# Issuing the transposes of an older attention block ahead of the new block's logits

## The chip, the cores and the metric

The kernel runs on one core of one Trainium2 chip. The metric is device microseconds (us) of one execution. Names of engines: PE is the matrix engine (PEld its weight loads), DVE the vector engine, ACT the scalar engine, POOL the GpSimd engine, SP the engine that issues most DMAs.

## The reference

Two layers of a streaming encoder over 2048 tokens of width 1024. Layer 0 is a pooling mixer; one key/value projection follows it; layer 1 is attention with 16 heads of width 64. The change lies in the attention, which is not a softmax but "stick-breaking": a logit gives the chance to stop at a key, and the weight of a key is that chance times the product of (1 - chance) over all later keys.

```python
def stick_breaking_attention(q, k, v):
    # A[t,s] = beta[t,s] * prod_{s<j<t} (1 - beta[t,j]), beta = sigmoid(q.k / sqrt(d))
    ...
        log_keep = jnp.where(mask, jax.nn.log_sigmoid(-logits), 0.0)
        later = lax.cumsum(log_keep, axis=log_keep.ndim - 1, reverse=True) - log_keep
        log_a = jax.nn.log_sigmoid(logits) + later
        a = jnp.where(mask, jnp.exp(log_a), 0.0)
        outs.append(jnp.einsum('bhts,bhsd->bhtd', a.astype(v.dtype), v[:, :, :L]))
```

After it come the gate `o * silu(z)`, the output projection, and a gated embedding add.

## The kernel before

**Two stages.** The first stage (all dense layers up to q, k and v, and the copies of the later weights to DRAM in split form) ends at about 1410 us of the span; the change does not touch it. The second stage is the attention with the dense work that is left.

**Attention blocks.** The sequence is cut into four chunks of 512 tokens. The list `slots` runs over query chunks c from 3 down to 0, over 16 heads, and over key chunks from c down to 0. A slot is a 512x512 block of one head: 64 slots for c=3, 48 for c=2, 32 for c=1 and 16 for c=0. The slot with equal query and key chunk is called diagonal; there only the causal part is worked on. A slot has four steps, one for each 128 query rows, so there are 640 steps, counted by n from 0.

**What a step issues.** The loop at L809 to L842 issues four things for a step n:

- `front` (L591), the logits of step n: two matmuls (L598, L599) into a `psl` buffer, ACT's sigmoid (L602) into a `kap` buffer; in a diagonal slot POOL's causal select (L604) on it. `front` hands back `scan`: DVE's running product over the keys (L609), which writes `pp`.
- `turn` (L617), the transposes of the block that is `LAG_T` = 6 steps back: up to four transposes on PE (L623) of the `pp` tiles into a `psa` buffer, ACT's copy (L626), and DVE's subtraction (L627) that gives the rest of the split (`at`). It works on four scans of an earlier slot at a time, so its latest input is the scan three steps back.
- the filler: pieces of the dense products that are left (`piecewise`, L661: matmuls L664, L666, L668), `rate` of them per step: 3 with c=3, then 441/176, 441/112 and 441/48 for c=2, 1 and 0. Behind a finished product stand DVE, ACT and POOL instructions (L705 to L708, L729 to L732, L751 to L756).
- `gather` (L630), for the block `LAG_G` = 8 steps back: two matmuls (L635, L636) of `at` with v into `pso`; at the end of a head an ACT copy, a DVE addition, and for every second head a multiplication on POOL (L640 to L648).

**Buffers.** The product tiles lie in PSUM with two buffers for each of `psl`, `psa`, `pso` and `psd`. So the transposes of one step have to wait until the subtraction L627 of two steps earlier has read its `psa` buffer.

**Order.** Each engine works through its own queue in order. The tile framework's scheduler sets the order in each queue at build time: it starts from the order in which the code issues instructions, and lets one go ahead of another where it reckons that this one is ready sooner. What stands in the queues can be printed from the built program.

Of the kernel before, what the change touches and what calls it, by code (L numbers as in the profile page):

```python
# [29 lines left out]
def f(ap):  # L30
    return ap.bitcast(F32)
# [3 lines left out]
def trunk_kernel(ctx, tc, x, p, a_norm, a_w_in, a_w_group, a_scale, a_w_out, kv_norm, w_kv,  # L35
# [509 lines left out]
    with ExitStack() as st:  # L545
# [45 lines left out]
        def front(st, j):  # L591

            w = (j + 1) * P if st["diag"] else W5
            r0 = W5 - w
            ps = psl.tile([P, W5], F32, tag="psl", name="psl")
            qs = slice(j * P, (j + 1) * P)
            (qa, qb), kk = st["q"], st["k"]
            T.matmul(ps[:, :w], qa[:, qs], kk[:, :w], start=True, stop=False)  # L598
            T.matmul(ps[:, :w], qb[:, qs], kk[:, :w], start=False, stop=True)  # L599
            kp = kaps[kcount[0] % NK]  # L600
            kcount[0] += 1
            A.activation(out=kp[:, r0:], in_=ps[:, :w], func=AF.Sigmoid, scale=-1.0)  # L602
            if st["diag"]:
                G.affine_select(out=kp[:, W5 - P :], in_=kp[:, W5 - P :], pattern=[[-1, P]], compare_op=ALU.is_gt,  # L604
                                fill=1.0, base=0, channel_multiplier=1)

            def scan():
                pp = t2.tile([P, W5], F32, tag="pp", name="pp", bufs=12)
                V.tensor_tensor_scan(out=pp[:, r0:][:, ::-1], data0=kp[:, r0:][:, ::-1],  # L609
                                     data1=zeros.to_broadcast([P, w]),  # L610
                                     initial=1.0 if st["diag"] else st["carry"][j], op0=ALU.mult, op1=ALU.add)
                st["carry"][j] = pp[:, r0 : r0 + 1]
                st["a"].append((pp, r0))

            return scan

        def turn(st, kt):  # L617

            j0 = kt if st["diag"] else 0
            pt = psa.tile([P, W5], F32, tag="psa", name="psa")  # L620
            for j in range(j0, 4):
                pp, r0 = st["a"][j]
                T.transpose(pt[:, j * P : (j + 1) * P], pp[:, r0 + kt * P : r0 + (kt + 1) * P], ident)  # L623
            at = t2.tile([P, 2, W5], F32R, tag="at", name="at", bufs=3)
            cs = slice(j0 * P, W5)
            A.copy(out=at[:, 0, cs], in_=pt[:, cs])  # L626
            V.tensor_tensor(out=at[:, 1, cs], in0=pt[:, cs], in1=f(at[:, 0, cs]), op=ALU.subtract)  # L627
            st["at"][kt] = at

        def gather(st, kt):  # L630
            cs = slice((kt if st["diag"] else 0) * P, W5)
            if st["diag"] and kt == 0:
                st["o"].append(pso.tile([P, W5], F32, tag="pso", name="pso"))
            po, at, vv = st["o"][0], st["at"].pop(kt), st["v"]
            T.matmul(po[:, cs], vv[:, kt, :], at[:, 0, cs], start=(st["diag"] and kt == 0), stop=False)  # L635
            T.matmul(po[:, cs], vv[:, kt, :], at[:, 1, cs], start=False, stop=(st["last"] and kt == 3))  # L636
            if st["last"] and kt == 3:
                half, os, c, h2 = st["h"] % 2, st["os"], st["c"], st["h"] // 2
                mine, other = slice(half * HD, (half + 1) * HD), slice((1 - half) * HD, (2 - half) * HD)
                A.copy(out=os[mine], in_=po[other])  # L640
                V.tensor_tensor(out=os[mine], in0=po[mine], in1=os[mine], op=ALU.add)  # L641
                if half:
                    zt = t2.tile([P, W5], F32, tag="zt", name="zt", bufs=1)
                    nc.sync.dma_start(out=zt, in_=zd[c][h2])
                    for j in range(4):
                        js = slice(j * P, (j + 1) * P)
                        A.activation(out=os[:, js], in_=os[:, js], func=AF.Identity, bias=ends[c][:, h2, j : j + 1])  # L647
                    G.tensor_tensor(out=os, in0=os, in1=zt, op=ALU.mult)  # L648
                    outs[c].append(os)
# [127 lines left out]
        def beside(c):  # L777

            if c < NSUB - 1:
                yield from post(c + 1)  # L780
                return
            for cz in range(c, -1, -1):
                yield from gate_z(cz)
# [3 lines left out]
        slots = []  # L787
# [4 lines left out]
        active, filler, owed, head = {}, beside(NSUB - 1), 0.0, {}  # L792
        rate = POSTZ / 64.0
        LAG_T, LAG_G = 6, 8
# [3 lines left out]
        def begin(i):  # L798
            c, h, kc = slots[i]
            if kc == c:  # L800
                if h == 1:
                    ends[c] = load_ends(c)
                os = head["os"] if h % 2 else t2.tile([P, W5], F32, tag="os", name="os", bufs=9)
                head.clear()
                head.update(q=load_q(c, h), carry=[None] * 4, o=[], os=os)
            kk, vv = load_kv(kc, h)
            active[i] = dict(head, c=c, h=h, k=kk, v=vv, diag=kc == c, last=kc == 0, a=[], at={})

        for n in range(4 * len(slots) + LAG_G):  # L809
            i, j = divmod(n, 4)  # L810
            scan = None
            if i < len(slots):
                c, h, kc = slots[i]
                if j == 0:
                    if i == 0:
                        begin(0)
                    if i + 1 < len(slots):
                        begin(i + 1)
                scan = front(active[i], j)
            i2, j2 = divmod(n - LAG_T, 4)  # L820
            if 0 <= i2 < len(slots):
                turn(active[i2], j2)
            if scan is not None:
                scan()
            owed += rate
            while owed >= 1.0:
                next(filler, None)
                owed -= 1.0
            i3, j3 = divmod(n - LAG_G, 4)
            if 0 <= i3 < len(slots):  # L830
                gather(active[i3], j3)
                if j3 == 3:
                    st3 = active.pop(i3)
                    c3 = st3["c"]
                    if len(outs[c3]) == 8 and c3 not in done:
                        done.add(c3)
                        for _ in filler:
                            pass
                        if c3:
                            filler = beside(c3 - 1)  # L840
                            rate = POST / (64.0 * c3 - 2 * LAG_G)
                            owed = 0.0  # L842
# [31 lines left out]
```

## Time and profile before

| | before |
|---|---|
| median of 3 runs | 2869.15 us (2866.77 to 2869.49) |
| the profiled execution | 2867.54 us |
| its span | 2865.7 us |
| PE busy, share of the span | 96% |
| DVE busy | 66% (about nine tenths in the first two thirds of the attention) |
| ACT busy | 49% |
| POOL busy | 33% |
| DMA, mean | 201 GB/s |

The profile is one execution, with an instruction's start and duration on each engine. The time of a group of instructions can be added up for a stretch of the span; for a wait the profile names the instruction whose end released it. Matmuls overlap each other: the end of one is modelled, and lies after the start of the next.

### The profile page before, as it was taken

The page shows a single profiled execution, that of the slowest core. Times are in us where ns is not written, and L with a number is a line of the kernel's source. Part 1 is how long each engine was busy: PE and PEld are TensorE (multiplying, and loading weights), DVE is VectorE, ACT ScalarE, POOL GpSimd, SP SyncE. Part 2 cuts the span into 40 slices and gives each one's busy share as a digit, 9 for nine tenths or more (in the row PEclk, how much of TensorE's full clock was granted, in tenths as well). Part 3 has the DMA queues.
Part 4 walks back from the last instruction along what each step waited for, and adds up shares of the span by engine and source line. Part 5 has one row for each costly group of instructions (what it writes and reads, how often), then busy time and mean ns, then how long its engine had stood idle before and what let it go on. Part 6 is the DMA issues. An engine that isn't in the chain of part 4 may idle for free. (4 is left out here: it accounts for less than half of the span.)

```text
span 2865.7 us, 40527 instructions
## 1 busy us (share of the span) xinstructions
PE 2763.3 (96%) x13667; PEld 2273.2 (79%) x13667; DVE 1893.8 (66%) x2581; ACT 1405.6 (49%) x2765; POOL 956.2 (33%) x965
## 2 busy tenths in 40 slices
PE   8899999999999999999899999999999999999999
PEld 6688788888888888888777888787877778878877
DVE  5645535455355543555299989999999988886642
ACT  4444523355234542345255555656566655554431
POOL 3464347542474425743212121221111122213220
PEclk9999999999999999999999999999999999999999
DMA  7756696467955678446657565555555556667765
GB/s 265 257 162 216 220 305 208 143 205 250 306 160 169 223 243 287 136 153 207 212 188 229 163 216 170 159 164 177 165 161 161 163 176 193 186 188 243 251 207 158
DMA packets 335139, 576.43 MB, mean 201 GB/s; under 512 B 32782, under 2 KB 161838, under 8 KB 334932
## 3 DMA queue, kind: packets, MB, share of 16 engines
q1 hardware_dynamic: 327944, 564.34, 61.2%
q10 hardware_dynamic: 6988, 9.50, 1.1%
q8 instruction: 108, 1.77, 0.3%
q14 instruction: 99, 0.81, 0.1%
HBM read 433.16 MB, written 132.19 MB: 197 GB/s over the span
## 5 line engine op out<-in xcount | busy, mean ns | idle before, releaser
L353 PE MATMUL psd<-wpair,x 128*128 128x512 f32 x2304 | 544.8, 393 | 0.0
L602 ACT ACTIVATE kap<-psl 128x512 f32<-128x512 f32 (+3 forms) x640 | 340.3, 533 | 407.6 <-PE psl L599 398.3
L609 DVE TENSOR_TENSOR_SCAN pp<-kap,pp,zeros 128x512 f32<-128x512 f32 x384 | 512.2, 1338 | 23.3 <-ACT kap L602 21.2
L353 PEld LDWEIGHTS psd<-wpair,x 128*128 128x128 f32 x2304 | 428.8, 188 | 86.4
L623 PE MATMUL psa<-ident,pp 128*128 128x128 f32 x2176 | 348.7, 275 | 42.7 <-DVE at L627 37.9
L627 DVE TENSOR_TENSOR at<-psa,at 128x512 fp32r<-128x512 f32 (+3 forms) x640 | 373.5, 586 | 14.8 <-ACT at L626 13.8
L623 PEld LDWEIGHTS psa<-ident,pp 128*128 128x128 f32 x2176 | 263.5, 141 | 127.0 <-DVE at L627 71.2
L626 ACT CAST at<-psa 128x512 fp32r<-128x512 f32 (+3 forms) x640 | 331.3, 519 | 51.7 <-PE psa L623 48.5
L604 POOL TENSOR_SCALAR_AFFINE_SELECT kap<-kap 128x128 f32<-128x128 f32 x256 | 88.0, 345 | 633.1 <-ACT kap L602 597.9
L609 DVE TENSOR_TENSOR_SCAN pp<-kap,zeros 128x128 f32<-128x128 f32 (+3 forms) x256 | 214.2, 838 | 93.7 <-POOL kap L604 92.4
L598 PE MATMUL psl<-kk,qa 128*128 128x512 f32 (+3 forms) x640 | 235.0, 367 | 7.0 <-ACT vr L390 5.2
L635 PE MATMUL pso<-at,vv 128*128 128x512 f32 (+3 forms) x640 | 235.2, 367 | 0.8 <-ACT at L626 0.7
L599 PE MATMUL psl<-kk,qb 128*128 128x512 f32 (+3 forms) x640 | 235.1, 367 | 0.0
L636 PE MATMUL pso<-at,vv 128*128 128x512 f32 (+3 forms) x640 | 234.1, 366 | 0.0
L126 PE MATMUL psd<-xp,wpair 128*128 128x512 f32 x512 | 201.2, 393 | 4.3 <-DVE wpair L108 4.2
L124 PE MATMUL psd<-xp,wpair 128*128 128x512 f32 x512 | 201.0, 393 | 3.6 <-ACT xp L169 2.4
L108 DVE SCALAR_TENSOR_TENSOR wpair<-wraw,gains,wpair 128x512 fp32r<-128x512 f32 x192 | 149.5, 790 | 82.1 <-ACT wpair L107 81.8
L125 PE MATMUL psd<-xp,wpair 128*128 128x512 f32 x512 | 200.7, 392 | 0.0
L107 ACT ACTIVATE wpair<-wraw,gains 128x512 fp32r<-128x512 f32 x192 | 136.8, 720 | 121.0 <-DMA wraw<-in_w_kv_dram 65.9
L103 POOL TENSOR_TENSOR wpair<-wraw,wpair 128x512 fp32r<-128x512 f32 x107 | 147.7, 1388 | 78.5 <-ACT wpair L101 58.8
L101 ACT CAST wpair<-wraw 128x512 fp32r<-128x512 f32 x160 | 96.1, 619 | 124.1 <-DMA wraw<-in_a_w_out_dram 51.5
L598 PEld LDWEIGHTS psl<-kk,qa 128*128 128x128 f32 x640 | 120.9, 189 | 28.7 <-ACT vr L390 5.7
(204 smaller groups left out, 5553.4 us busy)
## 6 DMA issues: line engine op xcount, KB each, us to landing
wpair<-wi SPq DMA_DIRECT2D x96, 512.0 KB
kk<-kd SPq DMA_DIRECT2D x320, 128.0 KB
vv<-vd SPq DMA_DIRECT2D x160, 256.0 KB
wraw<-in_w_kv_dram SPq DMA_DIRECT2D x128, 256.0 KB
wpair<-wzd SPq DMA_DIRECT2D x64, 512.0 KB
wpair<-wod SPq DMA_DIRECT2D x64, 512.0 KB
wpair<-wgd SPq DMA_DIRECT2D x64, 512.0 KB
wi<-wpair SPq DMA_DIRECT2D x32, 512.0 KB
```

What stands on the lines that cost most here:

```text
L124: T.matmul(ps, wst(units, kt, 0, c0), acts[kt][:, 0], start=(kt == order[0]), stop=False)
L126: T.matmul(ps, wst(units, kt, 1, c0), acts[kt][:, 0], start=False, stop=(kt == order[-1]))
L353: T.matmul(pss2[i], ck["x2"][kt][:, xh, tk], wst(ws, kt, wh, 0, W5), start=(kt == 0 and xh == 0 and wh == 0), stop=(kt == KT - 1 and wh == 1))
L598: T.matmul(ps[:, :w], qa[:, qs], kk[:, :w], start=True, stop=False)
L599: T.matmul(ps[:, :w], qb[:, qs], kk[:, :w], start=False, stop=True)
L602: A.activation(out=kp[:, r0:], in_=ps[:, :w], func=AF.Sigmoid, scale=-1.0)
L609: V.tensor_tensor_scan(out=pp[:, r0:][:, ::-1], data0=kp[:, r0:][:, ::-1], data1=zeros.to_broadcast([P, w]), initial=1.0 if st["diag"] els ...
L623: T.transpose(pt[:, j * P : (j + 1) * P], pp[:, r0 + kt * P : r0 + (kt + 1) * P], ident)
L626: A.copy(out=at[:, 0, cs], in_=pt[:, cs])
L627: V.tensor_tensor(out=at[:, 1, cs], in0=pt[:, cs], in1=f(at[:, 0, cs]), op=ALU.subtract)
L635: T.matmul(po[:, cs], vv[:, kt, :], at[:, 0, cs], start=(st["diag"] and kt == 0), stop=False)
L636: T.matmul(po[:, cs], vv[:, kt, :], at[:, 1, cs], start=False, stop=(st["last"] and kt == 3))
```

## The change

The call of `turn` moves up, from behind `front` to ahead of it. Nothing else is edited.

```diff
         for n in range(4 * len(slots) + LAG_G):
+            i2, j2 = divmod(n - LAG_T, 4)
+            if 0 <= i2 < len(slots):
+                turn(active[i2], j2)
             i, j = divmod(n, 4)
             scan = None
             if i < len(slots):
...
                 scan = front(active[i], j)
-            i2, j2 = divmod(n - LAG_T, 4)
-            if 0 <= i2 < len(slots):
-                turn(active[i2], j2)
             if scan is not None:
                 scan()
             owed += rate
```

Each queue has as many attention instructions as before. In the two stretches below a row is one instruction of the built program, with its line, its output and inputs, and its shape.

The first is PE's queue in the middle of chunk c=3 (`psl` are logits, `psa` the transposes, `psd` a filler product, `pso` the product with v). It is a piece of the difference, - for before and + for the change.

```order
+L623 MATMUL psa<-ident,pp 128x128 x4
+L598 MATMUL psl<-kk,qa 128x512
+L599 MATMUL psl<-kk,qb 128x512
 L664 MATMUL psd<-x_19793,wpair 128x512
 L666 MATMUL psd<-x_19793,wpair 128x512
 L635 MATMUL pso<-at,vv 128x512
 L636 MATMUL pso<-at,vv 128x512
-L598 MATMUL psl<-kk,qa 128x512
-L599 MATMUL psl<-kk,qb 128x512
-L623 MATMUL psa<-ident,pp 128x128 x4
```

Within a step the four transposes and the two logit matmuls change places; filler and gather stay. Of the 634 steps that have both, the transposes stand first in 3 before and in 598 after; the rest lie at the start of the attention, where query chunks change, and at its end.

The second is DVE's queue at the end of a head in c=3 (L609 is a scan, L627 the subtraction that follows the transposes, L705 and L685 belong to fillers, L641 to the end of a head). Before:

```order
L609 SCALAR_TENSOR_TENSOR pp<-kap_12856,pp,zeros 128x512
L627 TENSOR_TENSOR at<-psa,at 128x384
L705 TENSOR_TENSOR zr<-psd,rb 128x512
L641 TENSOR_TENSOR os<-pso,os 64x512
L627 TENSOR_TENSOR at<-psa,at 128x256
L609 SCALAR_TENSOR_TENSOR pp<-kap_12853,pp,zeros 128x512
L609 SCALAR_TENSOR_TENSOR pp<-kap_12854,pp,zeros 128x512
L627 TENSOR_TENSOR at<-psa,at 128x128
```

and in the change:

```order
L627 TENSOR_TENSOR at<-psa,at 128x384
L609 SCALAR_TENSOR_TENSOR pp<-kap_12856,pp,zeros 128x512
L705 TENSOR_TENSOR zr<-psd,rb 128x512
L641 TENSOR_TENSOR os<-pso,os 64x512
L627 TENSOR_TENSOR at<-psa,at 128x256
L609 SCALAR_TENSOR_TENSOR pp<-kap_12853,pp,zeros 128x512
L627 TENSOR_TENSOR at<-psa,at 128x128
L609 SCALAR_TENSOR_TENSOR pp<-kap_12854,pp,zeros 128x512
```

Before, the scan of a step stands ahead of that step's subtraction in 542 of the 634 steps; in the change the subtraction stands first in 618. ACT's copies (L626) and sigmoids (L602) change places in the same way: the copy stood first in 1 step, and stands first in 607. In POOL's queue some seven instructions change places with a neighbour, and in SP's queue some weight loads and loads of v.

## The prediction

> **What bounds the kernel now.** I read the busy shares first, then the busy times of the four query chunks, then PE's waits in each, then the timeline of single steps. The page's busy line says that PE sets the span:
>
> ```profile
> PE 2763.3 (96%) x13667; PEld 2273.2 (79%) x13667; DVE 1893.8 (66%) x2581; ACT 1405.6 (49%) x2765; POOL 956.2 (33%) x965
> ```
>
> That is a mean over two stages. The busy times of the attention by chunk, c=3, 2, 1 and 0 (start:end, length, then busy time and instructions of each engine, the granted clock, DMA), with the switches between chunks left out:
>
> ```profile
> core 0: us, PE busy (x) PEld busy (x) DVE busy (x) ACT busy (x) POOL busy (x), PEclk, DMA share, GB/s
> 1450.00:1940.00 490.00, 475.83 (x2591) 395.60 (x2590) 448.98 (x540) 286.24 (x570) 101.42 (x97) 1.00 0.59 183
> 1945.00:2310.00 365.00, 347.71 (x1899) 281.53 (x1899) 341.92 (x427) 225.73 (x461) 56.79 (x85) 1.00 0.54 164
> 2330.00:2570.00 240.00, 233.73 (x1280) 194.24 (x1279) 206.19 (x273) 139.00 (x303) 52.29 (x81) 1.00 0.64 192
> 2590.00:2735.00 145.00, 144.93 (x767) 122.80 (x767) 87.25 (x139) 66.84 (x162) 42.62 (x69) 1.00 0.80 255
> ```
>
> With c=0 PE never stops. With c=3 and c=2 DVE is nearly as full as PE (449 of 490 us, 342 of 365 us), and each loses time to the other. PE's waits (total, times, longest) with c=3:
>
> ```profile
> PE psa L623 <- DVE at L627: 13.1, 12, 2.0
> ```
>
> with c=2:
>
> ```profile
> PE psa L623 <- DVE at L627: 13.0, 22, 1.8
> PE psao L761 <- DVE sg L756: 2.2, 1, 2.2
> PE psae L586 <- DVE at L627: 0.8, 1, 0.8
> ```
>
> and with c=1:
>
> ```profile
> PE psa L623 <- DVE at L627: 2.3, 5, 0.6
> ```
>
> So PE loses time at one place: the transposes wait for a `psa` buffer, which the subtraction of two steps earlier (L627, on DVE) gives back. A steady step with c=3, from the timeline (start, duration, engine):
>
> ```profile
> 1707.32 0.39 PE L599 MATMUL psl<-kk,qb 128*128 128x512 f32 x1
> ...
> 1707.55 0.60 PE L623 MATMUL psa<-ident,pp 128*128 128x128 f32 x4
> 1707.74 0.60 ACT L602 ACTIVATE kap<-psl 128x512 f32<-128x512 f32 x1 [0.98 <-PE psl L599]
> ...
> 1707.90 0.48 PE L664 MATMUL psd<-xz,wpair 128*128 128x512 f32 x1
> ...
> 1708.21 0.66 DVE L627 TENSOR_TENSOR at<-psa,at 128x512 fp32r<-128x512 f32 x1
> ...
> 1708.24 0.58 ACT L626 CAST at<-psa 128x512 fp32r<-128x512 f32 x1
> ...
> 1708.80 1.27 DVE L609 TENSOR_TENSOR_SCAN pp<-kap,pp,zeros 128x512 f32<-128x512 f32 x1
> ...
> 1709.61 0.60 PE L623 MATMUL psa<-ident,pp 128*128 128x128 f32 x4
> ...
> 1709.99 0.66 DVE L627 TENSOR_TENSOR at<-psa,at 128x512 fp32r<-128x512 f32 x1
> ...
> 1711.67 0.60 PE L623 MATMUL psa<-ident,pp 128*128 128x128 f32 x4
> ```
>
> A step takes PE 2.06 us (1707.55 to 1709.61) and DVE 1.78 (1708.21 to 1709.99): 1.19 for the scan, 0.59 for the subtraction. L599 is given 0.39 us, though the next PE instruction starts 0.23 after it, so a wait costs about 0.16 more than the idle time shown: 13.1 + 12 x 0.16 = 15.0 us with c=3, 16.0 + 24 x 0.16 = 19.8 with c=2, 2.3 + 5 x 0.16 = 3.1 with c=1.
>
> The transposes of 1707.55 have been copied by about 1708.8 (1708.24 + 0.58), when DVE comes free. But DVE takes the scan first and subtracts at 1709.99, until 1710.58. The transposes that need this buffer come at 1711.67: **1.1 us of slack**. When DVE gets extra work, the slack is gone. The largest wait with c=3:
>
> ```profile
> 1698.84 1.29 POOL L708 TENSOR_TENSOR zr<-zr,sgz 128x512 f32<-128x512 f32 x1 [11.68 <-DMA qb<-qd]
> 1699.14 4.23 DVE L609 TENSOR_TENSOR_SCAN pp<-kap,pp,zeros 128x512 f32<-128x512 f32 x2
> ...
> 1700.16 2.13 POOL L648 TENSOR_TENSOR os<-os,zt 128x512 f32<-128x512 f32 x1
> ...
> 1700.47 0.24 ACT L626 CAST at<-psa 128x128 fp32r<-128x128 f32 x1
> ...
> 1703.29 0.26 DVE L627 TENSOR_TENSOR at<-psa,at 128x128 fp32r<-128x128 f32 x1
> ...
> 1703.61 0.66 PE L623 MATMUL psa<-ident,pp 128*128 128x128 f32 x4 [2.03 <-DVE at L627]
> ```
>
> Two scans beside POOL's multiplications take 4.23 us instead of 2 x 1.19, and a subtraction whose copy was done at 1700.71 stands behind both of them.
>
> **The change part by part.** No instruction is added or taken away. On PE the four transposes and two logit matmuls change places. From one step's transposes to the next PE has the same work, so no wait moves by that alone; four transposes hold back their successor for 0.35 us (1707.55 to 1707.90) whether that is a filler or a logit matmul. I cost it at nothing.
>
> What counts is that the scheduler turns DVE's and ACT's queues round as well. DVE now subtracts before it scans in 618 of 634 steps (before: 92), ACT copies before its sigmoid in 607. In the steady step the subtraction would start at 1708.8 and end at 1709.4, which leaves 2.3 us of slack instead of 1.1: one scan more.
>
> What the move makes late is the sigmoid: its logits start 0.35 us later, and its copy goes first. It has cover: ACT idles 0.98 us ahead of it in each step, and behind it the scan now waits for a subtraction that ends after the sigmoid. With the cover gone it costs up to 0.35 us a step. In diagonal slots POOL's select stands in between and the cover is thin. DVE's waits there, with c=3 and then with c=2:
>
> ```profile
> DVE pp L609 <- POOL kap L604: 31.5, 32, 1.5
> ```
>
> ```profile
> DVE pp L609 <- POOL kap L604: 12.1, 24, 1.0
> DVE sg L756 <- POOL sg L755: 7.5, 7, 1.4
> ```
>
> With c=3 they lie in DVE's own spare time (41 us); with c=2 DVE has 23 us to spare. Transposes and logits issue no DMA, the loads that change neighbours in SP's queue stay within a slot, and PE's waits above hold none on DMA: nothing. POOL's few swaps: nothing.
>
> The sum by chunk:
>
> - **c=3.** In the wait shown PE came to the transposes at 1703.61 - 2.03 = 1701.58. With the subtraction between the two scans its buffer is free about halfway through the 4.23 us, near 1701.5: no wait. The next subtraction then follows the second scan, 1703.37 + 0.26 + 0.58 = 1704.2, for transposes that come at 1701.58 + 2.06 = 1703.6: 0.6 us of wait stays. The mean of the 12 waits is 1.1 us, less than the 1.19 us that move out of the way. Leaving about 0.2 us on each, 15.0 - 2.5 = **12.5 us** go; bounds 0 and 15.0.
> - **c=2.** Here DVE ends the gain. Its 341.9 us of work stay, and the 7.5 us for POOL in L756. The 12.1 us for the select vanish while DVE is behind and stay when it is not; I keep half. 341.9 + 7.5 + 6.1 = 355.5 us for what took 365: **9.5 us** go. Bounds: 0, and 365 - 349.4 = 15.6.
> - **c=1.** All its waits are below 1.19 us: **3 us**; bounds 0 and 3.1.
> - **c=0 and the switches between chunks.** PE does not wait with c=0, and around the switches the queues keep the old order: 0. Bounds there are taken as 3 us either way, a little over the longest single wait shown (2.2).
>
> Together 25 us. Against the profiled execution that is 2867.5 - 25 = 2842.5; the median of the runs lies 1.6 us above it (2869.15 against 2867.54), so **2844 us**.
>
> A check with the Trainium skill. Beside POOL two scans lost 4.23 - 2.38 = 1.85 us. The page "SBUF — State Buffer" (section "Who interferes with whom") has it that a DVE instruction with two SBUF inputs and a GpSimd instruction that reads SBUF lock each other out for a whole instruction, and that a DVE instruction with one SBUF input is not touched. The trace fits: the scan has two (`kap` and `zeros`), and one that is held until POOL ends at 1702.29 and then needs about 1.1 us gives the 1703.37 shown. By that rule the 0.26 us subtraction, which reads PSUM and one SBUF input, would run inside the locked time, and each such place would be 0.26 us better than in my sum, 1.8 us for seven of them; by durations as the rows show them, nothing.
>
> **The rivals.**
>
> *DVE is the limit and the wait only moves.* The 1.85 us lost beside POOL and all other DVE work stay. If they come back as waits one step later, as the 0.6 us above does, only the short waits go: 3 us, 2866. For it: with c=2 DVE has 94% of the stretch. Against it: with c=3 DVE gains 0.28 us on PE in each steady step, 4.5 in the 16 steps of a head.
>
> *The logits come too late: slower.* Logits now stand behind transposes that wait, and in diagonal slots sigmoid, select and scan follow each other. If each of the 64 diagonal steps with c=2 made DVE wait 0.35 us more, c=2 would take 341.9 + 7.5 + 12.1 + 22.4 = 383.9 us, 18.9 longer; less 12.5 and 3 from the other chunks, 3.4 us slower: 2872.5. It decides when the select costs DVE more than about 31 us with c=2 (365 + 15.5 - 349.4), against 12.1 now. Against it: the subtraction that used to follow the wait now fills it.
>
> *The scheduler undoes the move.* It would be 2869, but the built queues show the move, so this has no chance of its own.
>
> **How the numbers follow.** The forecast, with half to all of the bounded gain, 15 to 34 us, has 0.70. A gain of 6 to 15, where c=2 or c=3 gives little, has 0.10. The first rival has 0.13, the second 0.07. A measurement of this kernel tells about 0.2% (5.7 us) from no change. So faster 0.80, same 0.13, slower 0.07. The range reaches from all bounds met, 15.0 + 15.6 + 3.1 + 3 = 36.7 or 2832, to 2865, within the first rival's few microseconds.
>
> **What would show it.** Right, if PE's waits at L623 for DVE fall below 4 us with c=3 and below 8 with c=2, if PE's busy share there rises and DVE's with it, and if subtractions follow their copies at once. Wrong in size, if with c=2 DVE shows new waits for POOL's select or the sigmoid. Wrong in its mechanism, if the transposes still wait as long while subtractions stand ahead of the scans, or if the scans lose more time beside POOL than now.

## The result and the profile after

| | before | changed |
|---|---|---|
| median | 2868.58 us (4 runs, 2866.77 to 2869.49) | 2841.23 us (4 runs, 2839.86 to 2843.22) |
| ratio | | 0.991, 95% interval 0.9897 to 0.9922 |
| span of the profiled execution | 2865.7 us | 2839.6 us |

The change makes the kernel 27 us faster; 25 had been forecast. The busy times of the changed kernel, from the page:

```profile
PE 2754.7 (97%) x13667; PEld 2272.8 (80%) x13667; DVE 1896.1 (67%) x2581; ACT 1408.5 (50%) x2765; POOL 952.6 (34%) x965
```

The work is the same; the holes in it are fewer. By chunk, with the stretches laid to the chunks' new places (start:end, length, then busy time and instructions of PE, PEld, DVE, ACT and POOL, the granted clock, DMA share, GB/s):

```profile
1445.00:1917.00 472.00, 465.37 (x2541) 387.75 (x2540) 444.16 (x530) 280.90 (x559) 88.73 (x96) 1.00 0.58 187
1946.00:2274.00 328.00, 321.71 (x1792) 266.95 (x1791) 316.77 (x401) 209.65 (x432) 58.90 (x84) 1.00 0.54 170
2301.00:2538.00 237.00, 232.60 (x1280) 194.94 (x1279) 206.76 (x272) 139.07 (x297) 52.47 (x78) 1.00 0.61 193
2565.00:2712.00 147.00, 146.22 (x776) 123.82 (x775) 88.62 (x140) 69.66 (x164) 44.42 (x70) 1.00 0.79 254
```

PE is idle for 6.6 us with c=3 (before 14.2) and for 6.3 with c=2 (before 17.3); DVE for 28 (before 41) and 11 (before 23). PE's waits at the transposes (total, times, longest) with c=3:

```profile
PE psa L623 <- DVE at L627: 6.0, 12, 1.0
```

and with c=2:

```profile
PE psa L623 <- DVE at L627: 4.3, 7, 1.0
```

for 13.1 and 13.0 before. DVE's own waits with c=2, where the select's were 12.1 and those of L756 7.5:

```profile
DVE sg L756 <- POOL sg L755: 3.5, 4, 1.1
DVE pp L609 <- POOL kap L604: 3.3, 6, 1.1
DVE at L627 <- ACT at L626: 1.8, 6, 0.5
```

A steady step of the changed kernel with c=3, from the timeline (start, duration, engine; in brackets the wait ahead of it):

```profile
1716.33 0.60 PE L623 MATMUL psa<-ident,pp 128*128 128x128 f32 x4
...
1716.97 0.59 ACT L626 CAST at<-psa 128x512 fp32r<-128x512 f32 x1 [0.98 <-PE psa L623]
...
1717.59 0.69 DVE L627 TENSOR_TENSOR at<-psa,at 128x512 fp32r<-128x512 f32 x1
...
1718.19 1.28 DVE L609 TENSOR_TENSOR_SCAN pp<-kap,pp,zeros 128x512 f32<-128x512 f32 x1
...
1720.44 0.60 PE L623 MATMUL psa<-ident,pp 128*128 128x128 f32 x4
```

The copy is done at 1717.56, the subtraction follows at once, ahead of the scan, and gives the buffer back at about 1718.2. It is wanted at 1720.44: 2.3 us of slack, where the step shown before had 1.1.

What is left with c=3 lies mostly at the end of every second head, as before: seven such places hold 3.9 of the 6.0 us. The longest, from the timeline:

```profile
1886.13 1.29 POOL L708 TENSOR_TENSOR zr<-zr,sgz 128x512 f32<-128x512 f32 x1 [10.45 <-DVE os L641]
1886.42 2.08 DVE L609 TENSOR_TENSOR_SCAN pp<-kap,pp,zeros 128x512 f32<-128x512 f32 x1
...
1887.44 2.14 POOL L648 TENSOR_TENSOR os<-os,zt 128x512 f32<-128x512 f32 x1
...
1888.42 0.26 DVE L627 TENSOR_TENSOR at<-psa,at 128x128 fp32r<-128x128 f32 x1
1888.61 2.06 DVE L609 TENSOR_TENSOR_SCAN pp<-kap,pp,zeros 128x512 f32<-128x512 f32 x1
1888.91 0.46 PEld L623 LDWEIGHTS psa<-ident,pp 128*128 128x128 f32 x4
...
1890.59 0.66 DVE L685 TENSOR_TENSOR og<-os,og 128x512 fp32r<-128x512 f32 x1
...
1891.17 0.68 DVE L627 TENSOR_TENSOR at<-psa,at 128x512 fp32r<-128x512 f32 x1
...
1891.91 0.66 PE L623 MATMUL psa<-ident,pp 128*128 128x128 f32 x4 [0.96 <-DVE at L627]
```

The subtraction of 0.26 us now stands between the two long scans, and the transposes of 1889.0 no longer wait for it. The next ones do, by 0.96 us: DVE was held up twice by POOL and had a filler's instruction (L685) to do as well.

### The profile page after: what moved, and what is told of

It is laid out like the page before. It is cut to its first block, busy times and chain, and to the rows that moved or that the text cites. A ratio compares the mean times of both kernels' runs of the same rounds, so it can differ in the third digit from the quotient of the medians.

```text
span 2839.6 us, 40404 instructions
## 1 busy us (share of the span) xinstructions
PE 2754.7 (97%) x13667; PEld 2272.8 (80%) x13667; DVE 1896.1 (67%) x2581; ACT 1408.5 (50%) x2765; POOL 952.6 (34%) x965
## 5 line engine op out<-in xcount | busy, mean ns | idle before, releaser
L626 ACT CAST at<-psa 128x512 fp32r<-128x512 f32 (+3 forms) x640 | 333.0, 521 | 406.4 <-PE psa L623 400.5
L609 DVE TENSOR_TENSOR_SCAN pp<-kap,pp,zeros 128x512 f32<-128x512 f32 x384 | 511.2, 1332 | 4.6 <-ACT kap L602 2.5
L627 DVE TENSOR_TENSOR at<-psa,at 128x512 fp32r<-128x512 f32 (+3 forms) x640 | 379.2, 594 | 59.5 <-ACT at L626 56.8
L602 ACT ACTIVATE kap<-psl 128x512 f32<-128x512 f32 (+3 forms) x640 | 343.5, 538 | 15.5 <-PE psl L599 7.2
L598 PE MATMUL psl<-kk,qa 128*128 128x512 f32 (+3 forms) x640 | 281.3, 440 | 6.7 <-ACT vr L390 5.5
L609 DVE TENSOR_TENSOR_SCAN pp<-kap,zeros 128x128 f32<-128x128 f32 (+3 forms) x256 | 213.5, 835 | 40.4 <-POOL kap L604 37.2
L635 PEld LDWEIGHTS pso<-at,vv 128*128 128x128 f32 x640 | 120.2, 188 | 28.1 <-ACT at L626 2.6
```

## The experiments

Theory A: the gain comes from DVE's order, which follows from the move. B: it comes from PE's order itself. C: from ACT copying before its sigmoid. Each ratio below is against runs of the kernel before on the same chip. The end of the dense stage, which no kernel here touches, differs by up to 10 us between executions, so I also give the length of the attention in the profiled execution: the span less the start of the first sigmoid L602. Profiles of the same order differ in it by up to 2 us (the changed kernel has 1407.3 and 1409.2, e1 and its two repeats 1401.1 to 1401.6). For the kernel before and the changed one the first sigmoid starts at

```profile
L602 ACT ACTIVATE kap<-psl x640: 270/597/660, 1431.9 to 2747.7; 128x512 f32<-128x512 f32 x96, 128x128 f32<-128x128 f32 x64
```

```profile
L602 ACT ACTIVATE kap<-psl x640: 277/598/657, 1432.3 to 2721.5; 128x512 f32<-128x512 f32 x96, 128x128 f32<-128x128 f32 x64
```

which gives 1433.8 us before and 1407.3 in the changed kernel. In the table "first" means first within a step, counted in the built queues over 634 steps.

| kernel | transposes first (PE) | copy first (ACT) | subtraction first (DVE) | median us | ratio (95%) | attention us |
|---|---|---|---|---|---|---|
| before | 3 | 1 | 92 | 2868.58 | 1 | 1433.8 |
| changed | 598 | 607 | 618 | 2841.23 | 0.991 (0.9897 to 0.9922) | 1407.3 |
| e1_dve_alone | 3 | 1 | 634 | 2832.76 | 0.9879 (0.9864 to 0.9894) | 1401.1 |
| e3_dve_and_act | 4 | 634 | 634 | 2834.7 | 0.9886 (0.9871 to 0.9901) | 1405.8 |
| e6_after_pinned | 593 | 602 | 634 | 2839.8 | 0.9906 (0.9891 to 0.9922) | 1406.2 |
| e2_dve_undone | 568 | 577 | 0 | 2904.96 | 1.0136 (1.0121 to 1.0151) | 1475.4 |
| e9_pe_alone | 571 | 0 | 0 | 2901.65 | 1.0123 (1.0108 to 1.0139) | 1469.5 |

**DVE's order alone** (e1_dve_alone): the kernel before, each scan pinned (`keep_in_program_order`) behind the DVE instruction that stands ahead of it in the code, the subtraction.

```diff
-                V.tensor_tensor_scan(out=pp[:, r0:][:, ::-1], data0=kp[:, r0:][:, ::-1],
-                                     data1=zeros.to_broadcast([P, w]),
+                tc.keep_in_program_order(V.tensor_tensor_scan(
+                    out=pp[:, r0:][:, ::-1], data0=kp[:, r0:][:, ::-1], data1=zeros.to_broadcast([P, w]),
...
```

> The kernel before, with each scan pinned behind the subtraction of its step on DVE (634 of 634 steps); PE and ACT keep the order of before. Theory A (DVE's order gives the gain, since the psa buffer is given back one scan earlier): 2840 to 2848 us, and PE's waits for DVE at the transposes fall as in the changed kernel. Theory B (the gain comes from PE reaching the transposes ahead of the logits): 2866 to 2871. Theory C (it comes from ACT copying ahead of the sigmoid): 2866 to 2871.

2832.76 us, 7 below what A expected: the whole gain and more, with logits ahead of transposes as before. B and C alone are out. PE's wait for DVE at the transposes, in the whole span, falls from

```profile
PE psa L623 <- DVE at L627: 37.9, 51, 2.0
```

before to

```profile
PE psa L623 <- DVE at L627: 16.0, 38, 1.2
```

and in the changed kernel it is

```profile
PE psa L623 <- DVE at L627: 20.9, 41, 1.3
```

**The change without DVE's part** (e2_dve_undone): the changed kernel, the subtraction pinned behind the scan.

```diff
-            V.tensor_tensor(out=at[:, 1, cs], in0=pt[:, cs], in1=f(at[:, 0, cs]), op=ALU.subtract)
             st["at"][kt] = at
+            def rest():
+                tc.keep_in_program_order(
+                    V.tensor_tensor(out=at[:, 1, cs], in0=pt[:, cs], in1=f(at[:, 0, cs]), op=ALU.subtract))
+            return rest
...
                 scan()
+            if rest is not None:
+                rest()
```

> The changed kernel, with each subtraction pinned behind the scan of its step on DVE; the transposes stay ahead of the logits on PE and the copy ahead of the sigmoid on ACT in most steps. Theory A: the gain is gone, 2865 to 2880 us (the scan is also later than before, so it may be slower than the kernel before). Theories B and C: 2838 to 2846.

2904.96 us, 25 above the upper end of what A expected. The gain is gone, and the attention takes 42 us longer than before. Not all of this need be the move: the pin also puts the scan first in the 92 steps that had the subtraction first before, and no run separates the two. DVE's waits in the whole span; the select's were 92.4 and the sigmoid's 21.2 before:

```profile
DVE pp L609 <- POOL kap L604: 126.3, 137, 2.5
DVE pp L609 <- ACT kap L602: 33.5, 132, 0.8
```

The scan now waits for logits that come later, and the subtraction waits behind it. PE's waits at the transposes rise as well (L631 is the subtraction here):

```profile
PE psa L623 <- DVE at L631: 57.1, 112, 1.6
```

This is the slower rival of the prediction, in a kernel where the subtraction does not fill the wait.

**PE's order alone** (e9_pe_alone): as e2, with the copy (`rest(0)`) also pinned behind the sigmoid; `rest(1)` is the subtraction.

```diff
-            A.copy(out=at[:, 0, cs], in_=pt[:, cs])
...
+            if rest is not None:
+                rest(0)
             if scan is not None:
                 scan()
+            if rest is not None:
+                rest(1)
```

> Transposes ahead of logits on PE in 571 of 634 steps; ACT keeps the sigmoid ahead of the copy and DVE the scan ahead of the subtraction, in all steps. Theory A: no gain, 2868 to 2885, since the logits come 0.35 us later and each scan and subtraction with them; the rest of the loss of the run with DVE's part undone (2905) is then the copy's place ahead of the sigmoid. Theory B: 2838 to 2846.

2901.65 us, again above the range. With PE's order alone the attention is 36 us longer than before, with the same 92 steps turned; the copy's place adds 6 by one profile of each, and 3 by the medians. Steps with c=3 show why (DVE and PE rows of the timeline; L632 is the subtraction here):

```profile
1711.48 0.66 PE L623 MATMUL psa<-ident,pp 128*128 128x128 f32 x4 [0.58 <-DVE at L632]
...
1713.27 1.28 DVE L609 TENSOR_TENSOR_SCAN pp<-kap,pp,zeros 128x512 f32<-128x512 f32 x1
...
1714.47 0.67 DVE L632 TENSOR_TENSOR at<-psa,at 128x512 fp32r<-128x512 f32 x1
...
1715.64 0.60 PE L623 MATMUL psa<-ident,pp 128*128 128x128 f32 x4
```

The transposes of 1711.48 get their subtraction at 1714.47, until about 1715.06, and the buffer is wanted at 1715.64: 0.6 us of slack, against 1.1 in the step shown of the kernel before and 2.3 in that of the changed one. The same slack (from 0.59 us after a subtraction's start to the transposes two steps on), taken over the 157 steps of c=3 from step 12 to 243 that have four transposes, as have the two behind them, has a median of 1.1 us before, 1.6 in the changed kernel, 1.3 in e1, and 0.5 in both e2 and e9.

**DVE's and ACT's order, PE's as before** (e3_dve_and_act): e1 with the sigmoid moved behind the copy too.

```diff
             def scan():
+                tc.keep_in_program_order(
+                    A.activation(out=kp[:, r0:], in_=ps[:, :w], func=AF.Sigmoid, scale=-1.0))
...
```

> The kernel before, with both the scan pinned behind the subtraction and the sigmoid pinned behind the copy; PE keeps logits ahead of transposes. Theory A: within 4 us of the run with DVE's order alone. Theory B: 2866 to 2871 us. Theory C: 2838 to 2846, and clearly below the run with DVE's order alone.

2834.7 us, within 4 us of e1 as A expected. Its attention is 4.7 us longer than e1's (1405.8 against 1401.1).

**The change with every scan pinned** (e6_after_pinned): the edit of e1 in the changed kernel.

> The changed kernel with the scan pinned behind the subtraction in all 634 steps (618 before); transposes ahead of logits on PE. Theory A with a price for the move on PE and ACT: 2836 to 2843, above the run with DVE's order alone (2832.8), since the logits and the sigmoid come later. If the few steps left in the old order around the changes of chunk make the difference, 2829 to 2835.

2839.8 us and 1406.2 us of attention, about as the changed kernel: the 16 steps left in the old order make next to nothing. What e1 has over it is the old order on PE and ACT. How these 5 us of attention divide is not settled: by the attention of e3 nearly all belong to ACT's order, but by the medians e3 is only 2 us slower than e1. With c=3 the cost goes with PE's order: from the sigmoid of step 8 to that of step 248, e1, e3 and the two repeats of e1 below take 473.5 to 474.1 us, and the changed kernel, its repeat and e6 take 476.0 to 476.6.

**The changed kernel and e1 side by side** (e10_after_again, e13_dve_alone_again).

> The changed kernel as it is, to stand beside the next run on the same chip: 2838 to 2845 us.

> The kernel before with DVE's order alone, once more. If the move on PE and ACT costs time once DVE's order is right, as the spans of the attention had it (1401.1 us here, 1407.3 in the changed kernel, 1406.2 there with all scans pinned), this is 4 to 8 us below the changed kernel in the same call. If the difference of the first pair of runs came from the dense stage, whose end moved by 6 us between them, the two are within 3 us.

2838.97 us (2835.96 to 2843.78) against 2832.94 (2832.28 to 2833.39), ratios 0.9908 (0.9894 to 0.9923) and 0.9886 (0.9871 to 0.99). The runs do not overlap, and the attention takes 1409.2 against 1401.5 us. So what the move does on PE and ACT costs 6 to 8 us; the order that it provokes on DVE earns over 30. A further run, e12_cast_later, was to put ACT's casts off:

> The kernel before with DVE's order alone, and the casts of a finished pair of heads (L684) put off until the next pair is done, for the chunks above 0. ACT then no longer stands for POOL's multiplication with a copy behind it (18 us of such waits in 17 places). If these hold up copies that PE needs, 2 to 5 us below the run with DVE's order alone; if they are hidden, the same within 2 us.

Its edit altered no instruction's place in the attention, so it tells nothing of the casts and only repeats e1: 2830.53 us.

**More room in place of another order** (e4_third_psa, e5_after_psa3, e7_dve_and_psa3): three `psa` buffers, for which one of `psl` is given up, in the kernel before, in the changed one and in e1.

```diff
-        psl = st.enter_context(tc.tile_pool(name="psl", bufs=2, space=bass.MemoryType.PSUM))
-        psa = st.enter_context(tc.tile_pool(name="psa", bufs=2, space=bass.MemoryType.PSUM))
+        psl = st.enter_context(tc.tile_pool(name="psl", bufs=1, space=bass.MemoryType.PSUM))
+        psa = st.enter_context(tc.tile_pool(name="psa", bufs=3, space=bass.MemoryType.PSUM))
...
-                return psl.tile([P, W5], F32, tag="psl", name="psdt")
+                return psa.tile([P, W5], F32, tag="psa", name="psdt")
```

> The kernel before, its order kept as far as the scheduler does, with three psa buffers and one psl buffer (the tail's products take psa in place of psl). Theory A in its cause (room in psa is what PE lacks): the waits for DVE at the transposes go by another way, 2835 to 2850 us. If order and not room matters, 2864 to 2872. A single psl buffer costs nothing as long as the sigmoid ends before the next logits, and the waits at the logits show it otherwise.

> The changed kernel with three psa buffers and one psl buffer. The change left 20.9 us of PE's waits for DVE at the transposes, and 9 or so of these where a query chunk changes. If room in psa is still what is short, these go, 2825 to 2835 us. If DVE's work is the limit by now, or the single psl buffer costs as much as it did in the kernel before (20.5 us of waits for the sigmoid at the logits), 2838 to 2850.

> The kernel before with DVE's order alone (the faster of the runs) and three psa buffers, one psl buffer. If the two act on the same waits, the third buffer adds little: 2828 to 2838 us, with the waits at the transposes near 0 and new ones at the logits. If they add up, below 2825.

In the kernel before it gives 2846.43 us, ratio 0.9931 (0.9914 to 0.9947), though the subtraction stands first in only 118 steps: room in `psa` is what PE lacks. It is not free. PE's waits there, in the whole span:

```profile
PE psl L598 <- ACT kap L602: 20.5, 31, 2.0
...
PE psa L623 <- DVE at L627: 0.3, 1, 0.3
```

The waits at the transposes are gone; the single `psl` buffer brings new ones at the logits, against the guess that it would cost nothing. On top of DVE's new order it gives nothing, or costs time: 2841.4 us for the changed kernel (ratio 0.9923, 0.9901 to 0.9945) and 2848.74 for e1 (0.9939, 0.9925 to 0.9954), with 21.6 and 26.0 us of waits at the logits. The last is 16 us more than e1's own time and 11 above the range that I gave. Since every one of these kernels also loses a `psl` buffer, none shows what a third `psa` buffer alone would bring.

**POOL's multiplications on DVE** (e11_pool_to_dve), in the changed kernel:

```diff
-                G.tensor_tensor(out=zr, in0=zr, in1=sg, op=ALU.mult)
+                V.tensor_tensor(out=zr, in0=zr, in1=sg, op=ALU.mult)
...
-                    G.tensor_tensor(out=os, in0=os, in1=zt, op=ALU.mult)
+                    V.tensor_tensor(out=os, in0=os, in1=zt, op=ALU.mult)
```

> The changed kernel with the two multiplications L648 and L708 on DVE in place of POOL. If POOL's reads hold up the scans, the scans of 2.1 us in chunk c=3 are gone (none above 1.4 us there), and the mean of the 384 full scans falls to about 1.28 us; DVE then has 62 more instructions of about 0.7 us. What the scans lose now beside POOL, some 0.8 us a time, is about what the instruction itself costs, so the time moves little: 2836 to 2852. If POOL is not the cause, the scans stay at 2.1 us and the time rises to 2850 or more.

The full scans with c=3 (shortest, median and longest, in ns), in the changed kernel and then here:

```profile
L609 DVE TENSOR_TENSOR_SCAN pp<-kap,pp,zeros x180: 1255/1273/2081, 1444.1 to 1915.7; 128x512 f32<-128x512 f32 x180
```

```profile
L609 DVE TENSOR_TENSOR_SCAN pp<-kap,pp,zeros x181: 1255/1274/1285, 1443.9 to 1914.5; 128x512 f32<-128x512 f32 x181
```

The long scans are gone, so they were POOL's doing. The nine full scans above 1.4 us that stay lie in later chunks, and each ends 1.08 us after a subtraction that POOL still does (L732). The time is 2832.94 us, ratio 0.9884 (0.9869 to 0.9898), 3 us below the range I gave and 6 below the changed kernel measured beside it (2838.97). The attention takes 1399.2 us, 8 to 10 less than in the two profiles of the changed kernel, though DVE has 64 instructions more (0.66 to 0.69 us each). Not all of this need come from the scans: with c=1, where no scan of the changed kernel is held up by a multiplication that moves, the time falls by 3 us too, and ACT's cast L684 waits 5.9 us in all for the product, not 20.1. So what the shorter scans alone are worth is open. This edit together with e1's was not tried.

## Why the prediction was right, and where its sizes were off

**The mechanism held.** The buffer of the transposes is given back one scan earlier, because DVE now subtracts first. Shown three ways: DVE's order alone gives the gain, the move without it gives a loss, and more room without it gives part of the gain. Of the signs that I had set, PE's waits with c=2 fell below 8 us (4.3) and those with c=3 did not fall below 4 (6.0). The busy shares of PE and DVE rise in both chunks, and the full scans lose no more time beside POOL (mean of all 384: 1332 ns, before 1338).

**The terms by chunk**, from the starts of the sigmoids of steps 8, 248, 264, 440, 456 and 568, which cut off the switches:

| | forecast gain | measured |
|---|---|---|
| c=3 | 12.5 us | 485.5 - 476.6 = 8.9 |
| c=2 | 9.5 | 339.9 - 327.7 = 12.2 |
| c=1 | 3 | 239.6 - 237.6 = 2.0 |
| switches c=3/2, 2/1, 1/0 | 0 | 0.7 + 1.8 + 0.9 = 3.4 |
| the rest of the span | 0 | -0.4 |
| together | 25 | 26.1 |

*c=3 was mis-sized*: I left 0.2 us on each of the 12 waits, but 6.0 us of idle time stay, 0.5 on each. At the seven places beside POOL both scans are held up as before, and the wait moves to the next transposes. In the place that I worked out, 0.6 us was right (0.58 measured); 0.2 as a mean was too hopeful. Of the 3.6 us that are missing, some 2.5 go with PE's new order, for in e1, with the old one, c=3 takes 474.1 us and gains 11.4.

*c=2 was mis-sized the other way*: I kept half of the 12.1 us for the select, and 3.3 stayed. The likely reason is that the subtraction, which no longer stands behind the waiting scan, fills that time. L756's 7.5 us, taken as fixed, fell to 3.5.

*The move's own cost was put at nothing, and is not*: 6 us between the changed kernel and e1 side by side, 5 to 8 by the attention. In the steady step the cover that I named does hold: the scan starts at 1718.19, as soon as the subtraction is done. Where the cover fails, the runs show only in part. That the sum came out near was in part luck: this cost and too small a gain with c=3 were made up by c=2 and by the switches, which I had put at nothing. A slip beside this: half of the bounded gain (33.7 us) is 16.9, not the 15 that my likeliest band began with.

**The rule of the Trainium skill on the shared port** ("SBUF — State Buffer", "Who interferes with whom") agrees in the changed kernel: the second scan ends at 1890.67, 1.09 us after POOL's L648 (1887.44 + 2.14). The two scans take 4.25 us there (from 1886.42) with the subtraction of 0.26 us between them, and took 4.23 before without it. So nearly all of the subtraction lies inside the locked time, as the rule has it.

**The rivals.** The first, that waits only move, holds for part of c=3. The second, logits too late, is a real force: 36 to 42 us where the subtraction is kept behind the scan, some of it perhaps from the 92 turned steps. I had limited its price to the 64 diagonal steps with c=2; in e2 and e9 every chunk but c=0 is 8 to 17 us longer than before, because the late scan also delays the subtraction that PE waits for.

## What to carry to other kernels

When an engine waits for a buffer, look at what stands ahead of the instruction that gives it back, in the queue of the engine that runs it: a release that is ready should not stand behind long work that nobody waits for yet. An edit in the order of the code acts through the order that a scheduler builds in every queue, so compare all the queues, and try to pin only the one that matters: here the pin alone gave more than the move.

## What the runs showed of the hardware

A scan with two inputs in SBUF, one of them a single column read again for each element (`zeros`), is held until a multiplication or subtraction on POOL ends: 1.27 us become up to 2.1, and each of the 39 full scans above 1.4 us in the changed kernel ends 1.08 us after such an instruction. It works the other way too: the multiplication L648 takes 2.12 to 2.14 us at the seven places where it meets two of these scans, and mostly 1.3 elsewhere. Where such an instruction on POOL takes 1.3 us and the same on DVE about 0.7, moving it to the busier engine was worth 6 us.
